# Strassen groups of a two-layer MLP: low parts on VectorE, the square on ScalarE, blocks released one by one

## The chip, the core and the metric

One core of a Trainium2 chip runs the kernel as one program. The time is the device time of one execution in microseconds (us); the median of several executions stands for a kernel. The profile is of one further execution of the same program. Engines: PE is TensorE's matmul, PEld its weight load, DVE VectorE, ACT ScalarE, POOL GpSimd, SP the queue that issues the loads and stores.

## The reference, cut to what matters

A two-layer network works on 512 latent and 256 context tokens of width 1024. Each layer is a mixer (attention, convolution, a state-space part) and then an MLP with 4096 hidden columns. Layer 0 runs the MLP for both token sets, layer 1 for the latent tokens only. All is float32. The part that the change is about:

```
def squared_relu_mlp(t, w1, w2):
    return jnp.square(jax.nn.relu(t @ w1)) @ w2
...
        f_lat = squared_relu_mlp(modulate(rms_norm(h, g_pre_mlp), sh2, sc2), w_mlp_in[l], w_mlp_out[l])
...
            f_ctx = squared_relu_mlp(modulate(rms_norm(hc, g_pre_mlp), sh2c, sc2c), w_mlp_in[l], w_mlp_out[l])
```

The shifts, scales and gates of a layer ("conditioning") come from `c_act @ w_ada[l] + b_ada[l]`, with a matrix of 1024 x 6144.

## The kernel before

**Splitting.** Each float32 operand of a large product is split into a high part, rounded to the matmul's type by a ScalarE cast, and a low part, the difference, by a subtraction. Three matmuls (high-high, high-low, low-high; `mm3`, L638) then stand for one product.

**The MLP** (`phase_mlp`, L1435) takes the hidden columns in 8 groups of 512, which are 4 column blocks of 128. Groups 0 and 7 run plainly. Groups 1 to 6 of both layers (`E.fast`, L1005) run `strassen(g)` (L1457), in four stages:

1. `blocks` and `wload` (L629, L614) load the four blocks of w_mlp_in, two at a time, and split them. Of each two, the first low part is made on VectorE and the second on GpSimd (L624).
2. `up` (L1462) makes 24 matmuls for one block, then relu on ScalarE (L1468) and its square on VectorE (L1470). For context tokens a cast (L1472) and a subtraction (L1473) follow. In layer 0 the four blocks are gone through for the context tokens, and then again for the latent ones.
3. `w2_forms` (L653) loads four rows of w_mlp_out into raw tiles and makes eight forms in layer 0, seven in layer 1: quarters of the matrix, or differences of them (L666) that overwrite the raw quarters. `halves_split` (L644) makes a form's two halves: two casts (L648) and two low parts, one on VectorE and one on GpSimd (L649). `h_forms` (L687) makes seven forms of the hidden values (L696, L697, L703 to L709).
4. Seven products (`times`, L1500) of 12 matmuls each, with two additions to the accumulators after each (L1514). They come in the order l11 r11, l12 r21, s2 t2, s1 t1, s3 t3, s4 r22, l22 t4. In layer 0 the context tokens' plain product (L1488) stands among them.

**Buffers.** The tag "w" has 10 tiles of 4 KB a partition (`E.nw`, L996). Raw loads, split blocks and forms all take them, and so do the conditioning's raw loads (`ada_slice`, L817). In layer 1 the forms r22, t1 and t4, of two tiles each, have six tiles of their own, "wx" (L1454). Relu's output takes one of four tiles "t2", which transposes and the conditioning use too. The tag "B4" has two tiles in the MLP; the state-space preparation uses it in groups 1 to 3 of layer 0.

**Late conditioning.** In groups 4 and 5 of layer 0 two slices of layer 1's conditioning run: four steps after each two blocks of w_mlp_in (`E.ada1`, L1002). A step loads two tiles of 512 KB and makes eight matmuls on each (L825).

**Order.** The program is traced in source order. A scheduling pass then simulates it while it is built, and gives each engine and the SP queue a fixed order: what is ready first goes first, and among ready work what was traced first. At run time every queue keeps that order, and an instruction that waits holds up all that stand behind it on its engine. A tile's release is a wait of the same kind.

Of the kernel before, what the change touches and what calls it, by code (L numbers as in the profile page):

```python
# [7 lines left out]
F32 = mybir.dt.float32  # L8
# [3 lines left out]
AF = mybir.ActivationFunctionType  # L12
OP = mybir.AluOpType
# [597 lines left out]
    return E.wp.tile(shape, dt, name="w", tag="w", bufs=E.nw)  # L611


def wload(E, views):  # L614

    nc = E.nc
    raws, out = [], []
    for v in views:
        raws.append(wtile(E, [P, 1024]))
        nc.sync.dma_start(raws[-1], v)  # L620
    for turn, raw in enumerate(raws):
        hi, lo = (wtile(E, [P, 1024], F32R) for _ in range(2))
        nc.scalar.copy(hi, raw)  # L623
        (nc.gpsimd if turn % 2 and E.wpool else nc.vector).tensor_sub(lo, raw, hi.bitcast(F32))  # L624
        out.append((hi, lo))
    return out


def blocks(E, w, b0, n, k):  # L629

    return [[x.rearrange("p (k c) -> p k c", k=k) for x in hl] for hl in wload(E, [w[b0 + i] for i in range(n)])]


def w_out_load(E, l, half):
# [6 lines left out]
    nc.tensor.matmul(out, ll, rh, start=False, stop=last)  # L641


def halves_split(E, wt, src, turn):  # L644

    hi, lo = (wt([P, 2, 512], F32R) for _ in range(2))
    for i, x in enumerate(src):
        E.nc.scalar.copy(hi[:, i], x)  # L648
        (E.nc.gpsimd if (i + turn) % 2 else E.nc.vector).tensor_sub(lo[:, i], x, hi[:, i].bitcast(F32))  # L649
    return hi, lo  # L650


def w2_forms(E, views, ctx):  # L653


    nc = E.nc
    V = nc.vector
    raw = []
    for v in views:
        raw.append(wtile(E, [P, 1024]))  # L660
        nc.sync.dma_start(raw[-1], v)
    q = {(j, n): [raw[2 * j + i][:, n * 512:(n + 1) * 512] for i in range(2)] for j in range(2) for n in range(2)}

    def sub(o, x, y):
        for i in range(2):
            V.tensor_sub(q[o][i], q[x][i], q[y][i])  # L666

    F = {}
    wx = E.wx if E.nwx else lambda s, d: wtile(E, s, d)
    wt = lambda s, d: wtile(E, s, d)  # L670
    F["r11"] = halves_split(E, wt, q[0, 0], 0)
    F["r21"] = halves_split(E, wt, q[1, 0], 1)
    if ctx:
        F["r12"] = halves_split(E, wt, q[0, 1], 0)
    F["r22"] = halves_split(E, wx, q[1, 1], 1)
    sub((0, 0), (0, 1), (0, 0))
    sub((0, 1), (1, 1), (0, 1))
    sub((1, 1), (1, 1), (0, 0))
    F["t2"] = halves_split(E, wt, q[1, 1], 0)
    F["t1"] = halves_split(E, wx, q[0, 0], 1)  # L680
    sub((1, 0), (1, 0), (1, 1))
    F["t3"] = halves_split(E, wt, q[0, 1], 0)
    F["t4"] = halves_split(E, wx, q[1, 0], 1)
    return F


# [126 lines left out]
def ada_slice(E, a, M, l, s):  # L813
    nc = E.nc
    V = nc.vector
    for kc in range(8):
        raw = [wtile(E, [P, 1024]) for _ in range(2)]  # L817
        for k in range(2):
            c0 = s * 2048 + k * 1024
            nc.sync.dma_start(raw[k], a["w_ada"][l, kc * P:(kc + 1) * P, c0:c0 + 1024])  # L820
        if kc == 0:
            pa = E.pt('a')
        for k in range(2):
            for b in range(4):
                nc.tensor.matmul(pa[32 * b:32 * b + 32, k * 256:(k + 1) * 256], E.cT[:, kc],  # L825
                                 raw[k][:, b * 256:(b + 1) * 256], start=kc == 0 and k == 0, stop=kc == 7,
                                 skip_group_check=True)
        yield
    rows = E.t2([P, 512])
    nc.gpsimd.memset(rows, 0.0)  # L830
    bias = a["b_ada"][l, s * 2048:(s + 1) * 2048].rearrange("(o k b j) -> b o k j", o=1, k=2, b=4)
    for b in range(4):
        nc.sync.dma_start(rows[32 * b:32 * b + 2].rearrange("p (k j) -> p k j", k=2), bias[b].to_broadcast([2, 2, 256]))
    V.tensor_add(rows, rows, pa)
    pt = E.pt('a')
    for q in range(4):
        nc.tensor.transpose(pt[:, q * P:(q + 1) * P], rows[:, q * P:(q + 1) * P], E.ident)
    pv = pt.rearrange("p (k j b w) -> p k j b w", k=2, j=2, b=4)
    for w in range(2):
        V.tensor_copy(M.mod[s][:, w].rearrange("p (k b j) -> p k j b", k=2, b=4), pv[:, :, :, :, w])  # L840
    if s != 1:
        k = 0 if s == 0 else 1
        o = 8 if s == 0 else 0
        V.scalar_tensor_tensor(out=M.A[k], in0=M.mod[s][:, :, o:o + 8], scalar=1.0, in1=bc(M.gpre[:, k], 1, 2),
                               op0=OP.add, op1=OP.mult)
    if s != 0:
        k = s - 1
        gp = E.t2([P, 512])[:, :256]
# [142 lines left out]
def hybrid_kernel(tc, a, out):  # L991
# [40 lines left out]
def block(E, l, cols):  # L1032
# [13 lines left out]
    with psum_phase(E, f"m{l}", m=3, a=1, q=2) as E.pp, \  # L1046
            tc.tile_pool(name=f"mlp{l}", bufs=1, reuse_waits="tile") as E.g4p, \
            tc.tile_pool(name=f"prep{l}", bufs=1, reuse_waits="tile") as E.mp:
        E.ps, E.nb4 = 'a', 2
        E.xa = E.f4  # L1050
        a2 = phase_post(E, l, st)
        return phase_mlp(E, l, a2)


def drain(gen):
# [379 lines left out]
def phase_mlp(E, l, cols):  # L1435
# [15 lines left out]
    ada = ada_steps()  # L1451
    prep = ssm_spill(E) if l == 0 else iter(())

    E.nwx = 0 if both else 6  # L1454
    E.wx = lambda shape, dt: E.g4p.tile(shape, dt, name="wx", tag="wx", bufs=E.nwx)

    def strassen(g):  # L1457
# [4 lines left out]
        def up(c, w, sg):  # L1462
            n, A = (NL, aL) if sg == 0 else (NCX, aC)
            pt = E.pt('m')[:, :n]
            for kc in range(8):
                mm3(nc, pt, w[0][:, kc], w[1][:, kc], A(0, kc), A(1, kc), kc == 0, kc == 7)
            s = E.t2([P, 512])[:, :n]
            nc.scalar.activation(s, pt, AF.Relu)  # L1468
            o = s if sg else hf[c // 2][:, c % 2]
            V.scalar_tensor_tensor(out=o, in0=pt, scalar=0.0, in1=s, op0=OP.max, op1=OP.mult)  # L1470
            if sg:
                nc.scalar.copy(hx[0][:, c], s)  # L1472
                V.tensor_sub(hx[1][:, c], s, hx[0][:, c].bitcast(F32))  # L1473

        w = []
        for k in range(2):
            w.extend(blocks(E, w1, g * 4 + k * 2, 2, 8))
            for _ in range(E.ada1.get(g, 0)):
                next(ada, None)
        for _ in range(E.npr.get(g, 0)):  # L1480
            next(prep, None)
        for sg in ((1, 0) if both else (0,)):
            for c in range(4):
                up(c, w[c], sg)
        R = w2_forms(E, [w2[g * 4 + c] for c in range(4)], both)
        L = h_forms(E, hf)

# [40 lines left out]
    def mlp1(h1, c, w, sg, part=None):  # L1528
# [3 lines left out]
        pt = E.pt('m')[:, :n]  # L1532
        for kc in range(8):
            mm3(nc, pt, w[0][:, kc], w[1][:, kc], A(0, kc, ts), A(1, kc, ts), kc == 0, kc == 7)
        s = E.t2([P, 512])[:, :n]
        nc.scalar.activation(s, pt, AF.Relu)
        V.scalar_tensor_tensor(out=s, in0=pt, scalar=0.0, in1=s, op0=OP.max, op1=OP.mult)
        hi, lo = (h1[sg][q](c)[:, ts] for q in range(2))
# [120 lines left out]
```

## Time and profile before

| what | value |
|---|---|
| median of 3 executions | 1704.34 us (1702.84 to 1710.09) |
| the profiled execution's own time | 1707.07 us |
| span of its profile, first to last instruction | 1705.1 us |
| mean granted TensorE clock, as a share of full speed | 0.952 |
| Strassen groups of layer 0, from the span's start | about 500 to 948 us |
| Strassen groups of layer 1, from the span's start | about 1393 to 1645 us |

In the stretch view each engine has its busy time in the stretch and its number of instructions in brackets; PEclk is the granted clock's mean, and where it is below 1.00 a part of the stretch ran at half speed. In the views by line and in time order, the bracket or the last column is idle time of the engine just ahead of the instruction, and what ended it.

### The profile page before, as it was taken

To read this page: it belongs to the slowest core of one execution; us is meant where nothing else is said; L and a number is where in the kernel's file an instruction comes from. 1 tells how busy PE (TensorE), PEld (TensorE's weight loads), DVE (VectorE), ACT (ScalarE), POOL (GpSimd) and SP (SyncE) were. 2 spreads that over 40 slices of the span, in tenths; PEclk is the share of its full clock that TensorE was granted. 3 is DMA by queue.
4 is the path that set the end of the run, shared out by engine and by line. 5 is a ranking of instruction groups with operands and counts; after the bars stand their busy time and mean duration, and the time that the engine had idled before them with its cause. 6 is when DMAs were issued, how large, how long until landed. Compare 5 with 4: busy or idle time off the path is not lost.

```text
span 1705.1 us, 23175 instructions
## 1 busy us (share of the span) xinstructions
PE 1559.6 (91%) x8728; PEld 1249.1 (73%) x8728; DVE 1124.6 (66%) x2364; ACT 622.7 (37%) x1205; POOL 384.3 (23%) x297
## 2 busy tenths in 40 slices
PE   5999989997999999998999988999898999999997
PEld 2776866676888778676777866687676877777775
DVE  8676447758676974636366476743775658777775
ACT  5312245545413333323233344112554433334342
POOL 0000220122111222213132235003102233333332
PEclk9999999999899999999999998959899899999999
DMA  9465311033140412344420345731303222222232
GB/s 337 154 214 200 118 34 46 1 112 148 42 145 34 139 49 82 149 149 152 146 74 25 112 185 183 282 99 47 109 1 117 81 76 98 99 99 99 99 116 94
DMA packets 72991, 193.83 MB, mean 114 GB/s; under 512 B 15152, under 2 KB 25648, under 8 KB 72496
## 3 DMA queue, kind: packets, MB, share of 16 engines
q1 hardware_dynamic: 72880, 192.37, 32.5%
q8 instruction: 68, 1.11, 0.3%
q14 instruction: 43, 0.35, 0.1%
HBM read 172.15 MB, written 20.19 MB: 113 GB/s over the span
## 4 chain that ended last, share of the span: by engine, by line
PE 67%; DVE 20%; ACT 5%; DMA 4%; issue 2%; POOL 1%; SPq 0%; DVEq 0%; ACTq 0%; POOLq 0%
PE ps_m L639 14%; PE ps_m L640 13%; PE ps_m L641 13%; PE ps_q L1511 3%; PE ps_q L1510 3%; PE ps_q L1509 3%; PE ps_a L825 2%; ACT p L942 2%; PE ps_s L526 2%; PE ps_q L639 2%; DVE w L666 2%; DVE w L649 2%; PE ps_q L640 2%; PE ps_q L641 2%; PE ps_t L967 1%
## 5 line engine op out<-in xcount | busy, mean ns | idle before, releaser
L624 POOL TENSOR_TENSOR w<-w 128x1024 fp32r<-128x1024 f32 x55 | 137.9, 2508 | 376.0 <-ACT w L623 234.7
L623 ACT CAST w<-w 128x1024 fp32r<-128x1024 f32 x124 | 129.6, 1049 | 180.7 <-DMA w<-in_w_mlp_in 44.1
L639 PE MATMUL ps_m<-g,w 128*128 128x256 f32 (+1 forms) x544 | 183.1, 340 | 9.7 <-ACT w L623 3.8
L641 PE MATMUL ps_m<-g,w 128*128 128x256 f32 (+1 forms) x544 | 182.2, 336 | 1.6 <-DVE w L624 1.6
L640 PE MATMUL ps_m<-g,w 128*128 128x256 f32 (+1 forms) x544 | 182.8, 337 | 0.0
L649 POOL TENSOR_TENSOR w<-w 128x512 fp32r<-128x512 f32 x72 | 113.7, 1585 | 284.6 <-ACT w L648 277.9
L639 PE MATMUL ps_m<-f,w 128*128 128x512 f32 (+1 forms) x464 | 170.4, 370 | 1.0 <-DVE f L1140 0.6
L640 PE MATMUL ps_m<-f,w 128*128 128x512 f32 (+1 forms) x464 | 170.1, 367 | 0.0
L641 PE MATMUL ps_m<-f,w 128*128 128x512 f32 (+1 forms) x464 | 169.7, 366 | 0.0
L639 PE MATMUL ps_m<-w,f 128*128 128x512 f32 (+1 forms) x432 | 160.9, 376 | 8.9 <-DVE p L987 4.0
L641 PE MATMUL ps_m<-w,f 128*128 128x512 f32 (+1 forms) x432 | 161.1, 374 | 0.0
L640 PE MATMUL ps_m<-w,f 128*128 128x512 f32 (+1 forms) x432 | 160.0, 372 | 0.0
L1514 DVE TENSOR_TENSOR g<-g,ps_q 128x512 f32<-128x512 f32 x168 | 107.7, 680 | 58.0 <-PE ps_q L1511 57.9
L648 ACT CAST w<-w 128x512 fp32r<-128x512 f32 x144 | 82.4, 618 | 156.6 <-PE ps_m L640 75.0
L624 DVE TENSOR_TENSOR w<-w 128x1024 fp32r<-128x1024 f32 x69 | 84.2, 1222 | 67.3 <-ACT w L623 61.2
L639 PEld LDWEIGHTS ps_m<-g,w 128*128 128x128 f32 x544 | 107.9, 200 | 23.4 <-ACT w L623 4.8
L1510 PE MATMUL ps_q<-w,f 128*128 128x512 f32 x264 | 108.8, 412 | 11.5 <-DVE w L649 7.1
L641 PEld LDWEIGHTS ps_m<-g,w 128*128 128x128 f32 x544 | 108.0, 199 | 13.4 <-DVE w L624 2.7
L1511 PE MATMUL ps_q<-w,f 128*128 128x512 f32 x264 | 108.5, 411 | 8.8 <-DVE f L697 8.8
L640 PEld LDWEIGHTS ps_m<-g,w 128*128 128x128 f32 x544 | 108.4, 199 | 10.4 <-issue 1.2
L1509 PE MATMUL ps_q<-w,f 128*128 128x512 f32 x264 | 107.9, 410 | 7.5 <-ACT f L696 5.3
L649 DVE TENSOR_TENSOR w<-w 128x512 fp32r<-128x512 f32 x72 | 66.7, 926 | 60.5 <-ACT w L648 51.4
(316 smaller groups left out, 3372.2 us busy)
## 6 DMA issues: line engine op xcount, KB each, us to landing
w<-in_w_ada SPq DMA_DIRECT2D x88, 512.0 KB
w<-in_w_mlp_in SPq DMA_DIRECT2D x64, 512.0 KB
w<-in_w_mlp_out SPq DMA_DIRECT2D x64, 512.0 KB
w<-in_w_out SPq DMA_DIRECT2D x16, 512.0 KB
w<-in_w_conv SPq DMA_DIRECT2D x12, 512.0 KB
h_d<-g SPq DMA_DIRECT2D x12, 512.0 KB
w<-in_w_q SPq DMA_DIRECT2D x8, 512.0 KB
f<-h_d SPq DMA_DIRECT2D x8, 512.0 KB
```

What stands on the lines that cost most here:

```text
L526: nc.tensor.matmul(out(g), U[d].o[rows, q, k].rearrange("p t i -> p (t i)"), sp[d][rows, q, k, lo:NCH], start=False, stop=d == 1 and q == ...
L623: nc.scalar.copy(hi, raw)
L624: (nc.gpsimd if turn % 2 and E.wpool else nc.vector).tensor_sub(lo, raw, hi.bitcast(F32))
L639: nc.tensor.matmul(out, lh, rh, start=first, stop=False)
L640: nc.tensor.matmul(out, lh, rl, start=False, stop=False)
L641: nc.tensor.matmul(out, ll, rh, start=False, stop=last)
L648: E.nc.scalar.copy(hi[:, i], x)
L649: (E.nc.gpsimd if (i + turn) % 2 else E.nc.vector).tensor_sub(lo[:, i], x, hi[:, i].bitcast(F32))
L1509: nc.tensor.matmul(o, f[:, 0, c, js], rh[:, c], start=first and c == 0, stop=False, **kw)
L1510: nc.tensor.matmul(o, f[:, 0, c, js], rl[:, c], start=False, stop=False, **kw)
L1511: nc.tensor.matmul(o, f[:, 1, c, js], rh[:, c], start=False, stop=c == 1, **kw)
L1514: V.tensor_add(a_, a_, bank[:, th * 512:(th + 1) * 512])
```

## The change

All low parts of a Strassen group move from GpSimd to VectorE, those of w_mlp_in and those of the forms. The square of relu in a Strassen group is an ACT activation (Square) instead of a VectorE multiplication of the PSUM bank with relu's output. In layer 0, `up` goes block by block: context, then latent. Relu's output has two tiles "relu" of its own, in the plain groups also. The conditioning's raw loads in layer 0's MLP take the two "B4" tiles instead of "w" tiles. "wx" in layer 1 has four tiles instead of six.

```diff
-        (nc.gpsimd if turn % 2 and E.wpool else nc.vector).tensor_sub(lo, raw, hi.bitcast(F32))
+        (nc.gpsimd if turn % 2 and E.wpool and pool else nc.vector).tensor_sub(lo, raw, hi.bitcast(F32))
...
         E.nc.scalar.copy(hi[:, i], x)
-        (E.nc.gpsimd if (i + turn) % 2 else E.nc.vector).tensor_sub(lo[:, i], x, hi[:, i].bitcast(F32))
+        E.nc.vector.tensor_sub(lo[:, i], x, hi[:, i].bitcast(F32))
...
-        raw = [wtile(E, [P, 1024]) for _ in range(2)]
+        raw = [(E.ada_w or wtile)(E, [P, 1024]) for _ in range(2)]
...
         E.ps, E.nb4 = 'a', 2
+        E.ada_w = lambda E, shape: E.mp.tile(shape, F32, name="ada_w", tag="B4", bufs=E.nb4)
         E.xa = E.f4
         a2 = phase_post(E, l, st)
-        return phase_mlp(E, l, a2)
+        cols = phase_mlp(E, l, a2)
+        E.ada_w = None
+        return cols
...
-    E.nwx = 0 if both else 6
+    E.nwx = 0 if both else 4
...
-            s = E.t2([P, 512])[:, :n]
+            s = E.g4p.tile([P, 512], F32, name="relu", tag="relu", bufs=2)[:, :n]
             nc.scalar.activation(s, pt, AF.Relu)
             o = s if sg else hf[c // 2][:, c % 2]
-            V.scalar_tensor_tensor(out=o, in0=pt, scalar=0.0, in1=s, op0=OP.max, op1=OP.mult)
+            nc.scalar.activation(o, s, AF.Square)
...
-            w.extend(blocks(E, w1, g * 4 + k * 2, 2, 8))
+            w.extend(blocks(E, w1, g * 4 + k * 2, 2, 8, False))
...
-        for sg in ((1, 0) if both else (0,)):
-            for c in range(4):
-                up(c, w[c], sg)
+        for c in range(4):
+            if both:
+                up(c, w[c], 1)
+            up(c, w[c], 0)
...
-        s = E.t2([P, 512])[:, :n]
+        s = E.g4p.tile([P, 512], F32, name="relu", tag="relu", bufs=2)[:, :n]
```

## Rows read from the trace of the kernel before

**Rows 1.** The page's head and its busy times: busy us, share of the span.

```profile
span 1705.1 us, 23175 instructions
PE 1559.6 (91%) x8728; PEld 1249.1 (73%) x8728; DVE 1124.6 (66%) x2364; ACT 622.7 (37%) x1205; POOL 384.3 (23%) x297
```

**Rows 2.** Stretches of layer 0's Strassen groups: length, PE, PEld, DVE, ACT, POOL, PEclk, DMA, GB/s.

```profile
553.00:566.00 13.00, 8.79 (x39) 6.20 (x40) 13.00 (x19) 4.63 (x9) 4.71 (x3) 1.00 0.29 92
...
718.00:731.00 13.00, 9.65 (x70) 7.61 (x67) 2.50 (x4) 3.25 (x6) 2.52 (x1) 0.74 0.59 204
...
804.00:813.00 9.00, 6.39 (x45) 5.30 (x37) 1.68 (x3) 2.79 (x4) 2.38 (x1) 0.81 0.59 182
...
861.00:875.00 14.00, 10.62 (x33) 8.18 (x34) 7.32 (x13) 2.28 (x4) 5.39 (x3) 0.76 0.09 30
...
sum 448.00, PE 426.49 PEld 344.69 DVE 280.76 ACT 138.89 POOL 109.06; mean PE 47.39 PEld 38.30 DVE 31.20 ACT 15.43 POOL 12.12
```

**Rows 3.** Four groups of layer 1 as stretches: the undisturbed one, and their sum.

```profile
1540.80:1584.20 43.40, 41.48 (x181) 33.56 (x181) 34.67 (x48) 18.02 (x30) 15.37 (x10) 1.00 0.29 97
...
sum 178.40, PE 170.50 PEld 137.97 DVE 140.12 ACT 72.03 POOL 61.61; mean PE 42.62 PEld 34.49 DVE 35.03 ACT 18.01 POOL 15.40
```

**Rows 4.** PE's matmuls in order of time, inside a product: start, duration (us).

```profile
870.46 0.39 PE L1510 MATMUL ps_q<-w,f 128*128 128x512 f32 x1
...
870.69 0.39 PE L1511 MATMUL ps_q<-w,f 128*128 128x512 f32 x1
```

**Rows 5.** PE's waits from 500 to 948 us: total us, times, longest.

```profile
PE ps_q L1510 <- DVE w L649: 7.1, 9, 1.9
PE ps_q L1510 <- POOL w L649: 4.4, 3, 2.9
```

**Rows 6.** PE's waits from 1393 to 1645 us.

```profile
PE ps_q L1511 <- DVE f L697: 8.8, 7, 1.8
PE ps_q L1509 <- ACT f L696: 5.3, 6, 1.5
```

**Rows 7.** Groups by line and shape, whole trace: count, busy us, mean ns, idle ahead.

```profile
L649 POOL TENSOR_TENSOR w<-w 128x512 fp32r<-128x512 f32 x72 | 113.7, 1585 | 284.6 <-ACT w L648 277.9 <-DVE w L649 5.1 <-POOL w L649 1.1
...
L649 DVE TENSOR_TENSOR w<-w 128x512 fp32r<-128x512 f32 x72 | 66.7, 926 | 60.5 <-ACT w L648 51.4 <-DMA w<-in_w_mlp_out 6.1 <-POOL w L649 2.9
...
L624 DVE TENSOR_TENSOR w<-w 128x1024 fp32r<-128x1024 f32 x69 | 84.2, 1222 | 67.3 <-ACT w L623 61.2 <-PE ps_q L640 5.6 <-issue 0.3
...
L1470 DVE SCALAR_TENSOR_TENSOR f<-ps_m,t 128x512 f32<-128x512 f32 x48 | 32.7, 682 | 42.6 <-ACT t L1468 42.6
...
L717 ACT ACTIVATE dump<-f 128x512 bf16<-128x512 f32 x22 | 13.8, 627 | 3.2 <-DMA f<-in_ctx 2.6 <-DMA f<-in_x 0.5
```

**Rows 8.** In order of time: a GpSimd low part in layer 0, a VectorE difference in layer 1.

```profile
859.33 4.22 POOL L649 TENSOR_TENSOR w<-w 128x512 fp32r<-128x512 f32 x1
...
1503.17 2.64 DVE L705 TENSOR_TENSOR f<-f,f 128x512 f32<-128x512 f32 x1
```

**Rows 9.** The SP queue's loads ahead of the stretch from 718 us.

```profile
707.06 8.12 SPq L820 DMA_DIRECT2D w<-in_w_ada  x8
716.56 2.04 SPq L620 DMA_DIRECT2D w<-in_w_mlp_in  x2
```

**Rows 10.** PE waiting for a conditioning load near the start of the program.

```profile
51.72 0.64 PE L825 MATMUL ps_a<-w,cT 128*32 128x256 f32 x8 [1.19 <-DMA w<-in_w_ada]
```

**Rows 11.** A group's end in layer 1, order of time on ACT and DVE: relu, square, casts.

```profile
1493.06 0.59 ACT L1468 ACTIVATE t<-ps_m 128x512 f32<-128x512 f32 x1
...
1495.19 1.14 ACT L696 CAST f<-f 128x512 fp32r<-128x512 f32 x2
...
1493.98 0.68 DVE L1470 SCALAR_TENSOR_TENSOR f<-ps_m,t 128x512 f32<-128x512 f32 x1
```

**Rows 12.** The first relu of layer 0's plain group 0, and PE behind it.

```profile
432.57 0.66 ACT L1536 ACTIVATE t<-ps_m 128x256 f32<-128x256 f32 x2 [0.47 <-DVE f L785]
...
433.52 0.58 PE L639 MATMUL ps_m<-g,w 128*128 128x256 f32 x1 [1.58 <-DVE t L1537]
```

More of the change, by code (lines that the diff above doesn't have):

```diff
@@ L611, in wtile, with wload @@
     return E.wp.tile(shape, dt, name="w", tag="w", bufs=E.nw)
-def wload(E, views):
+def wload(E, views, pool=True):
     nc = E.nc
@@ L623, in wload, with blocks @@
         nc.scalar.copy(hi, raw)
-        (nc.gpsimd if turn % 2 and E.wpool else nc.vector).tensor_sub(lo, raw, hi.bitcast(F32))
+        (nc.gpsimd if turn % 2 and E.wpool and pool else nc.vector).tensor_sub(lo, raw, hi.bitcast(F32))
         out.append((hi, lo))
     return out
-def blocks(E, w, b0, n, k):
-    return [[x.rearrange("p (k c) -> p k c", k=k) for x in hl] for hl in wload(E, [w[b0 + i] for i in range(n)])]
+def blocks(E, w, b0, n, k, pool=True):
+    return [[x.rearrange("p (k c) -> p k c", k=k) for x in hl]
+            for hl in wload(E, [w[b0 + i] for i in range(n)], pool)]
 def w_out_load(E, l, half):
@@ L641, in mm3, with halves_split @@
     nc.tensor.matmul(out, ll, rh, start=False, stop=last)
-def halves_split(E, wt, src, turn):
+def halves_split(E, wt, src):
     hi, lo = (wt([P, 2, 512], F32R) for _ in range(2))
@@ L670, in w2_forms @@
     wt = lambda s, d: wtile(E, s, d)
-    F["r11"] = halves_split(E, wt, q[0, 0], 0)
-    F["r21"] = halves_split(E, wt, q[1, 0], 1)
+    F["r11"] = halves_split(E, wt, q[0, 0])
+    F["r21"] = halves_split(E, wt, q[1, 0])
     if ctx:
-        F["r12"] = halves_split(E, wt, q[0, 1], 0)
-    F["r22"] = halves_split(E, wx, q[1, 1], 1)
+        F["r12"] = halves_split(E, wt, q[0, 1])
+    F["r22"] = halves_split(E, wx, q[1, 1])
     sub((0, 0), (0, 1), (0, 0))
@@ L678, in w2_forms @@
     sub((1, 1), (1, 1), (0, 0))
-    F["t2"] = halves_split(E, wt, q[1, 1], 0)
-    F["t1"] = halves_split(E, wx, q[0, 0], 1)
+    F["t2"] = halves_split(E, wt, q[1, 1])
+    F["t1"] = halves_split(E, wx, q[0, 0])
     sub((1, 0), (1, 0), (1, 1))
-    F["t3"] = halves_split(E, wt, q[0, 1], 0)
-    F["t4"] = halves_split(E, wx, q[1, 0], 1)
+    F["t3"] = halves_split(E, wt, q[0, 1])
+    F["t4"] = halves_split(E, wx, q[1, 0])
     return F
@@ L1049, in block @@
         E.ps, E.nb4 = 'a', 2
+        E.ada_w = lambda E, shape: E.mp.tile(shape, F32, name="ada_w", tag="B4", bufs=E.nb4)
         E.xa = E.f4
         a2 = phase_post(E, l, st)
-        return phase_mlp(E, l, a2)
+        cols = phase_mlp(E, l, a2)
+        E.ada_w = None
+        return cols
 def drain(gen):
```

## The prediction

> **What bounds the kernel now.** I read the page first: TensorE is busy for 1559.6 of 1705.1 us, 91% [rows 1]. So only what takes away TensorE's waits, or its half-speed stretches behind them, can move the time, and at most there. I then read the Strassen groups as stretches.
>
> Layer 0's take 448.0 us with 426.5 of matmul, so 21.5 us are idle [rows 2]. Three stretches also ran partly at half clock. What half clock costs is the length times one minus PEclk: 13 x 0.26 = 3.4, 9 x 0.19 = 1.7 and 14 x 0.24 = 3.4 us, together 8.5. Layer 0 thus loses 30.0 us, in four parts:
> - 718 to 731: 3.35 idle and 3.4 clock; 804 to 813: 2.6 and 1.7. Together 11.1 us. Both follow a burst of loads: eight conditioning loads are issued from 707.06, and only at 716.56 the second two blocks of w_mlp_in [rows 9]. The conditioning had taken the w tiles.
> - 861 to 875: 3.4 idle and 3.4 clock, 6.8 us. TensorE waits for a GpSimd low part that took 4.22 us where their mean is 1.59 [rows 7, 8].
> - 553 to 566: 4.2 idle, and VectorE is busy for all 13.00 us [rows 2]. That is state-space preparation on top of a group.
> - the rest, 7.9 us, in pieces at the groups' ends. The list of waits names the low parts of forms: 7.1 us behind VectorE, 4.4 behind GpSimd, the 2.9 of the third part among them [rows 5].
>
> Four groups of layer 1 take 178.4 us, 44.6 each; the undisturbed one takes 43.4 with 41.5 of matmul at full clock [rows 3]. So a group loses 3.1 us: (178.4 - 170.5) / 4 = 2.0 idle, and 1.1 of clock. Six groups lose 18.6. The waits are the cast and the low part of a hidden form, at each group's end [rows 6].
>
> **The change, part by part.**
>
> *Low parts to VectorE.* 6 x 8 + 6 x 7 = 90 halves of forms and 24 blocks leave GpSimd. A half costs GpSimd 1.59 us and VectorE 0.93, a block costs VectorE 1.22 [rows 7]. So VectorE takes on 90 x 0.93 + 24 x 1.22 = 113 us at today's means. It gives up the squares: 48 x 0.68 = 33 us, and 24 of half the size, put at half of that, 8. Net +72 us, 6 a group. In layer 1 VectorE is busy 35.0 of 44.6 us [rows 3], so 41 would still fit. I expect less: its 0.93 and the 2.64 us of a difference [rows 8] fall while GpSimd works on the same tiles, and 0.68 is what the same shape takes on a PSUM operand [rows 7]. At 0.68 a half, all 180 halves cost 122 us, against some 90 x 0.93 = 84 for today's ninety, so 38 us more; with the blocks' 29 and the squares' -41 it is 26, two a group. Idle VectorE hides that, but not from 553 to 566, where there is none; for that part I take no gain.
>
> What goes is the GpSimd operation as the last link to a product. For the 861 to 875 hole I take 6.5 of 6.8. Of the 7.9 in pieces I take 3, because the forms still wait for tiles that earlier products hold, and that chain stays.
>
> The Trainium skill, SBUF — State Buffer, section Who interferes with whom, says that a VectorE instruction with two SBUF inputs and a GpSimd instruction that reads SBUF hold a shared port in turn, the second fully blocked. The 4.22 us agree with it. By that rule VectorE's long operations all go with GpSimd's, the whole 7.9 could go too, and the sum below would be 5 us lower; I keep to the rows, which show two such cases.
>
> *Square on ScalarE.* 48 squares at 0.63 us, the nearest row (a square of 128x512 from SBUF), plus 24 at half: 38 us more on an engine that is 37% busy [rows 1, 7], so hidden, but for the last of a group. There relu starts at 1493.06, VectorE's square at 1493.98 ends at 1494.66, and the cast starts at 1495.19 [rows 11], 2.13 us after relu. With the square on the same engine it can start after 0.59 + 0.63 = 1.2 us. The gain is 0.9 us a group at most; ScalarE's order can eat all of it, since casts of forms stand in the same queue.
>
> *Four wx tiles instead of six.* They hold r22, t1 and t4. With four, t4's casts wait for the end of the product s1 t1, and their raw tiles stay taken until then. t4 is wanted two products later: 24 matmuls at 0.23 us [rows 4] are 5.5 us, against two casts and two low parts, some 2.6. So t4 itself isn't late. But t3 then gets its tiles only from r11's, and the next group's first blocks load later by one form's splitting, 2 to 3 us. These blocks fill TensorE's time today while s2 is made. Fewer tiles can only delay, so the one bound is nothing; the other is a hole up to that load: 4.3 us idle and 1.7 of clock, against 3.1 today, +2.9 a group.
>
> For layer 1 I set 0.9 from the square and 1.1 from the low part and the clock against 1.0 for the tiles: -1.0 a group, -6 (bounds -18.6 and +17).
>
> *Blocks one by one.* In layer 0 the first block is free after its own 24 context and 24 latent matmuls rather than after the context pass over all four, and the last one at the same moment. No wait of rows 5 names these; I cost it at nothing, covered by the matmuls of the other blocks. It has no effect in layer 1.
>
> *Conditioning in B4 tiles.* The second two blocks no longer queue for tiles behind eight loads, so the 11.1 us should go. In exchange a conditioning load waits for the matmuls on the load two before, and TensorE, whose order is fixed, for the load. There are 32. Nearest row: 1.19 us waited for one such load [rows 10]. Bounds 0 and 32 x 1.19 = 38; with both loads of a step in flight, and two whole groups of other matmuls to spread them over (718 to 861 us today and more), I take 2. Net -9.
>
> *Relu tiles.* Group 0's first relu waits for a tile of the transposes, and TensorE 1.58 us behind it [rows 12]; layer 1 begins alike. Between 0 and -3.2; I take -1, as the square there stays behind VectorE's own queue.
>
> **Sum:** -6.5 - 3 - 6 - 9 - 1 = -25.5 us. The profiled execution's own time is 1707.07, 2.0 above its span and 2.7 above the median. That gives 1681.6 beside it, and 1678.8 beside the median of 1704.34. I say 1679.
>
> **Rivals.**
>
> *Layer 1 gives back what layer 0 gains.* The four wx tiles cost their full +2.9 a group, +17 us; layer 0 gains 18.5 and group 0 one. Net -2.5: 1702. For it: layer 1's holes sit just where a tile comes late. Against it: seven products of slack. The Trainium skill, Perfetto Trace Analysis, section Optimization Strategy, says that the same gap repeating on the engine that should be saturated can mean too few buffers for the next tile. By that rule the edit goes the wrong way in layer 1, where the gap does repeat [rows 3, 6]; no row shows six tiles against four. Chance 0.17.
>
> *Slower: the SP queue.* A conditioning load that waits for its B4 tile at the head of SP's queue holds every load behind it. Six times in groups 4 and 5 weights stand behind such loads (two pairs of w_mlp_in and the four of w_mlp_out in each). If each makes a hole as from 718 to 731, 6.75 us, they cost 40 instead of 11.1, so +29; with -16.5 from the other terms it is +13: 1717. It decides once a B4 tile comes free later than the load behind is wanted. Against it: a tile is held for eight matmuls of 0.64 us together [rows 10]. Chance 0.10.
>
> *The order isn't as meant.* The pass could still put conditioning first, and the 11.1 stay: -16, 1688. And VectorE may be full in the three preparation groups, +2 to +6 each: 1685 to 1697. Both lie on the faster side, in the forecast's 0.73.
>
> **How the numbers follow.** Some 0.5%, 8.5 us, is what a measurement of this kernel can tell from no change: faster is below 1695.8, slower above 1712.9. The forecast and its weaker forms have 0.73, the first rival 0.17, the second 0.10. At best all 30.0, 18.6 and 3.2 go, 1653, which I don't expect whole: low end 1657. The high end takes in the first rival: 1704.
>
> **What would show it.** Right: no GpSimd work in the Strassen stretches; halves at 0.68 us on VectorE; no hole behind the conditioning loads; PEclk 1.00 from 861 to 875's counterpart; layer 1's groups near 43.5 us. Wrong: TensorE waiting for conditioning loads or, in layer 1, for a VectorE difference, t4 or the next block; SP waiting on B4 in groups 4 and 5; groups of layer 1 above 45 us.

## The result, and the profile after

| | before | after |
|---|---|---|
| median (runs) | 1703.59 us (4: 1699.36 to 1710.09) | 1681.30 us (4: 1676.95 to 1683.63) |
| ratio, 95% interval | | 0.9863, 0.9824 to 0.9902 |
| profiled execution, its span | 1707.07, 1705.1 us | 1679.50, 1677.6 us |

The change is faster by 1.4%: 22 us between the medians, 27.5 between the two spans. The predicted 1679 lies 2.3 us beside the measured median. How the 27.5 us are composed is another matter, and most of what follows is about that.

The page of after, head and two groups of its costliest (line, engine, operation, count, busy us, mean ns, idle ahead):

```profile
span 1677.6 us, 22956 instructions
PE 1546.1 (92%) x8728; PEld 1235.4 (74%) x8728; DVE 1101.0 (66%) x2406; ACT 659.1 (39%) x1277; POOL 185.8 (11%) x183
...
L650 DVE TENSOR_TENSOR w<-w 128x512 fp32r<-128x512 f32 x144 | 93.5, 685 | 81.9 <-ACT w L649 81.9
```

GpSimd's work has halved [rows 1], and a half's low part takes VectorE 685 ns now instead of 926 [rows 7]. TensorE's busy time fell by 13.5 us although its 8728 matmuls are the same: the mean granted clock rose from 0.952 to 0.965.

To see where the time went I cut both spans at the same events: where the MLP begins (the mixer's last projection is copied out), the first and the last addition of a Strassen product, and the first projection of layer 1. In the stretch view (length, PE, PEld, DVE, ACT, POOL with instructions, PEclk, DMA, GB/s), the kernel before, and then after:

```profile
368.79:544.44 175.65, 162.79 (x921) 141.41 (x920) 121.42 (x321) 64.58 (x126) 37.28 (x29) 0.94 0.30 107
544.44:1048.75 504.31, 471.53 (x2472) 377.46 (x2470) 320.20 (x594) 169.81 (x303) 137.08 (x94) 0.97 0.33 115
1291.35:1405.87 114.52, 101.55 (x518) 85.75 (x516) 71.39 (x136) 45.26 (x83) 34.10 (x23) 0.93 0.26 94
1405.87:1705.10 299.23, 274.94 (x1164) 221.87 (x1164) 223.37 (x316) 111.08 (x183) 97.40 (x57) 0.97 0.29 101
```

```profile
367.64:532.76 165.12, 158.62 (x916) 138.86 (x915) 115.82 (x317) 66.90 (x132) 28.49 (x26) 0.98 0.32 114
532.76:1013.75 480.99, 465.40 (x2476) 372.44 (x2474) 312.38 (x609) 191.35 (x346) 39.10 (x36) 0.99 0.35 121
1251.38:1358.64 107.26, 98.76 (x517) 83.69 (x515) 70.13 (x137) 45.28 (x84) 20.91 (x14) 0.95 0.28 100
1358.64:1677.64 319.00, 280.32 (x1164) 223.10 (x1164) 215.71 (x344) 124.24 (x207) 18.77 (x11) 0.96 0.28 94
```

The four are the start of layer 0's MLP (with plain group 0), its Strassen groups with group 7 and the tail, the start of layer 1's MLP, and its Strassen groups to the end. They changed by -10.5, -23.3, -7.3 and **+19.8** us, together -21.3. The other 6.2 lie in mixers (1.2 and 0.1) and in layer 1's first projections (4.9), which the diff does not touch; in the kernels below those projections took anything from 89.9 to 98.2 us, so I put no cause to them.

TensorE's waits in the Strassen groups of after (total us, times, longest), layer 0 and then layer 1, against [rows 5, 6]:

```profile
PE ps_a L347 <- DVE f L341: 1.2, 1, 1.2
PE ps_q L1516 <- DVE w L650: 1.1, 1, 1.1
PE ps_m L640 <- ACT w L623: 0.6, 2, 0.4
...
PE ps_m L640 <- ACT w L623: 19.0, 6, 3.2
PE ps_q L1517 <- DVE f L698: 7.0, 6, 1.2
```

In layer 0 a few short waits are left, 2.9 us in all. In layer 1 a wait has appeared that the kernel before did not have there: six times, once a group, TensorE waits 3.2 us for the cast of the next block of w_mlp_in. A middle group as a stretch, and the sum of four:

```profile
1456.40:1504.30 47.90, 43.53 (x180) 34.49 (x180) 33.68 (x52) 20.26 (x33) 0.00 (x0) 0.96 0.26 88
...
sum 191.60, PE 174.05 PEld 138.52 DVE 135.26 ACT 80.85 POOL 0.00; mean PE 43.51 PEld 34.63 DVE 33.82 ACT 20.21 POOL 0.00
```

A group takes 47.9 us, 3.3 more than the mean of [rows 3]; (191.6 - 174.05) / 4 = 4.4 are idle, against 2.0. In order of time, on PE, ACT and the SP queue:

```profile
1451.55 0.39 PE L1515 MATMUL ps_q<-w,f 128*128 128x512 f32 x1
...
1462.20 0.50 PE L640 MATMUL ps_m<-g,w 128*128 128x512 f32 x1 [3.21 <-ACT w L623]
...
1452.57 0.59 ACT L1473 ACTIVATE relu<-ps_m 128x512 f32<-128x512 f32 x1
1453.19 0.63 ACT L1475 ACTIVATE f<-relu 128x512 f32<-128x512 f32 x1
1453.85 1.14 ACT L697 CAST f<-f 128x512 fp32r<-128x512 f32 x2
...
1461.10 1.04 ACT L623 CAST w<-w 128x1024 fp32r<-128x1024 f32 x1 [5.07 <-DMA w<-in_w_mlp_in]
...
1457.58 0.93 SPq L620 DMA_DIRECT2D w<-in_w_mlp_in  x2
```

Read it from the bottom: the load goes out at 1457.58, 6.0 us after the group's first product began (1451.55); the cast waits for it, and TensorE for the cast. What the load waits for is the low part of a form, as SP's waits from 1445 to 1460 us say:

```profile
SPq L620 <- DVE w L650: 23.3, 2, 23.1
```

The square and the cast behind relu come fast here: the cast starts 1.28 us after relu (1452.57 to 1453.85), so the 3.21 us are not its doing.

In the kernel before, the same load leaves at 1494.71, in a group whose last block's square starts at 1493.98 [rows 11]:

```profile
1494.71 0.80 SPq L620 DMA_DIRECT2D w<-in_w_mlp_in  x2
...
1498.00 1.05 ACT L623 CAST w<-w 128x1024 fp32r<-128x1024 f32 x1 [1.67 <-DMA w<-in_w_mlp_in]
```

There the cast starts 4.9 us after the relu of 1493.06; in after 8.5 us after the one of 1452.57. So the mechanism of my first rival happened in layer 1, while the total is that of the forecast. Something else must have paid for it, and the experiments had to find what.

### The profile page after: what moved, and what is told of

It is laid out like the page before. It is cut to its first block, busy times and chain, and to the rows that moved or that the text cites. A ratio compares the mean times of both kernels' runs of the same rounds, so it can differ in the third digit from the quotient of the medians.

```text
span 1677.6 us, 22956 instructions
## 1 busy us (share of the span) xinstructions
PE 1546.1 (92%) x8728; PEld 1235.4 (74%) x8728; DVE 1101.0 (66%) x2406; ACT 659.1 (39%) x1277; POOL 185.8 (11%) x183
## 4 chain that ended last, share of the span: by engine, by line
PE 72%; DVE 16%; ACT 5%; DMA 5%; issue 2%; POOL 1%; SPq 0%; DVEq 0%; ACTq 0%; POOLq 0%
PE ps_m L640 15%; PE ps_m L642 14%; PE ps_m L641 14%; PE ps_q L1515 4%; PE ps_q L1516 4%; PE ps_q L1517 4%; PE ps_a L826 3%; ACT p L943 2%; DMA w<-in_w_mlp_in 2%; PE ps_q L641 2%; PE ps_q L640 2%; PE ps_s L526 2%; PE ps_q L642 2%; DMA w<-in_w_ada 1%; DVE p L935 1%
## 5 line engine op out<-in xcount | busy, mean ns | idle before, releaser
L624 DVE TENSOR_TENSOR w<-w 128x1024 fp32r<-128x1024 f32 x93 | 115.6, 1244 | 113.1 <-ACT w L623 81.9
L624 POOL TENSOR_TENSOR w<-w 128x1024 fp32r<-128x1024 f32 x31 | 76.2, 2458 | 804.6 <-ACT w L623 422.4
L650 DVE TENSOR_TENSOR w<-w 128x512 fp32r<-128x512 f32 x144 | 93.5, 685 | 81.9 <-ACT w L649 81.9
L640 PEld LDWEIGHTS ps_m<-g,w 128*128 128x128 f32 x544 | 105.8, 197 | 38.6 <-ACT w L623 23.9
L642 PEld LDWEIGHTS ps_m<-g,w 128*128 128x128 f32 x544 | 107.2, 197 | 11.3 <-issue 1.2
L641 PEld LDWEIGHTS ps_m<-g,w 128*128 128x128 f32 x544 | 106.3, 196 | 12.3 <-issue 2.1
L1517 PE MATMUL ps_q<-w,f 128*128 128x512 f32 x264 | 104.5, 396 | 7.0 <-DVE f L698 7.0
L1515 PE MATMUL ps_q<-w,f 128*128 128x512 f32 x264 | 105.5, 402 | 0.6
L1516 PE MATMUL ps_q<-w,f 128*128 128x512 f32 x264 | 104.4, 395 | 1.2 <-DVE w L650 1.1
L640 PEld LDWEIGHTS ps_m<-f,w 128*128 128x128 f32 x464 | 89.1, 193 | 20.5 <-issue 6.6
```

The lines of the kernel that those rows point to most:

```text
L624: (nc.gpsimd if turn % 2 and E.wpool and pool else nc.vector).tensor_sub(lo, raw, hi.bitcast(F32))
L640: nc.tensor.matmul(out, lh, rh, start=first, stop=False)
L641: nc.tensor.matmul(out, lh, rl, start=False, stop=False)
L650: E.nc.vector.tensor_sub(lo[:, i], x, hi[:, i].bitcast(F32))
L1515: nc.tensor.matmul(o, f[:, 0, c, js], rh[:, c], start=first and c == 0, stop=False, **kw)
L1516: nc.tensor.matmul(o, f[:, 0, c, js], rl[:, c], start=False, stop=False, **kw)
```

## The experiments

All kernels compute the whole result. In the table each stretch is cut as above; ratios are to the kernel before on the same chip. Four of the kernels have the same code in layer 0 (after, wx6_relu1, wx6_t2, wx6_sq_dve): their layer 0 groups took 481.0, 481.8, 480.8 and 480.9 us, so a stretch repeats to about 1 us. Where a stretch is unchanged but scheduled anew, as layer 1's in the runs that edit layer 0 alone, it moves by up to 3; layer 1's first projections, above, move by 8.

| kernel | median us | ratio (95%) | start L0 | groups L0 | start L1 | groups L1 to end |
|---|---|---|---|---|---|---|
| before | 1703.59 | 1 | 175.6 | 504.3 | 114.5 | 299.2 |
| after | 1681.30 | 0.9863 (0.9824 to 0.9902) | 165.1 | 481.0 | 107.3 | 319.0 |
| wx6_relu1 | 1664.66 | 0.9756 (0.9727 to 0.9785) | 165.2 | 481.8 | 107.5 | 299.8 |
| wx6_t2 | 1668.37 | 0.9773 (0.9742 to 0.9804) | 165.1 | 480.8 | 110.4 | 302.1 |
| before_wx4 | 1742.62 | 1.0214 (1.0177 to 1.0252) | 175.6 | 505.4 | 115.1 | 336.3 |
| undo_relu | 1696.40 | 0.9946 (0.9914 to 0.9977) | 175.1 | 482.9 | 110.3 | 317.5 |
| undo_ada | 1678.40 | 0.9841 (0.9820 to 0.9863) | 165.1 | 479.4 | 108.7 | 317.7 |
| undo_order | 1687.44 | 0.9893 (0.9863 to 0.9922) | 166.2 | 483.9 | 108.9 | 317.7 |
| undo_pool | 1691.05 | 0.9921 (0.9893 to 0.9950) | 167.1 | 484.8 | 111.4 | 327.7 |
| undo_square | 1685.85 | 0.9883 (0.9861 to 0.9905) | 165.1 | 487.0 | 108.8 | 316.0 |
| undo_order_ada | 1690.28 | 0.9897 (0.9858 to 0.9936) | 167.7 | 495.6 | 107.3 | 316.1 |
| undo_order_ada_pool | 1705.76 | 0.9993 (0.9963 to 1.0023) | 166.6 | 498.4 | 111.6 | 323.6 |
| before_relu | 1685.35 | 0.9865 (0.9835 to 0.9895) | 167.2 | 500.6 | 110.6 | 297.7 |
| wx6_sq_dve | 1671.93 | 0.9793 (0.9764 to 0.9821) | 165.1 | 480.9 | 108.4 | 306.7 |

**1. Are the four wx tiles the hole in layer 1?** Six again in the changed kernel. To make room for them in layer 1, one run keeps a single relu tile there (no run has two beside six wx tiles), in both places where the tile is taken, and another takes relu's output from "t2" in layer 1, as before.

```diff
-    E.nwx = 0 if both else 4
+    E.nwx = 0 if both else 6
...
-            s = E.g4p.tile([P, 512], F32, name="relu", tag="relu", bufs=2)[:, :n]
+            s = E.g4p.tile([P, 512], F32, name="relu", tag="relu", bufs=2 if both else 1)[:, :n]
```

> The changed kernel with six wx tiles in layer 1 again; to make room, relu has one tile of its own there instead of two. Theory A (the four wx tiles make layer 1's longer groups: t4 waits for the end of the product s1 t1, its raw tiles stay taken, the next w_mlp_in load is issued 6.0 us after a group's first product instead of 2.7): the 3.2 us waits for a w_mlp_in cast go, layer 1's groups fall from 47.9 to 43 to 45 us, the kernel to 1657 to 1667 us. Theory B (the longer groups come from the low parts on VectorE and the square on ScalarE, which stand in those queues ahead of the next blocks): the groups stay near 47.9 and the time within 4 us of 1681.

```diff
-    E.nwx = 0 if both else 4
+    E.nwx = 0 if both else 6
...
-            s = E.g4p.tile([P, 512], F32, name="relu", tag="relu", bufs=2)[:, :n]
+            s = (E.g4p.tile([P, 512], F32, name="relu", tag="relu", bufs=2) if both else E.t2([P, 512]))[:, :n]
```

> The changed kernel with six wx tiles, and in layer 1 relu's output in the shared t2 tiles as before, so that layer 1's buffers are those of the kernel before. Theory A: groups of 43 to 45 us as in the other run with six. Theory C (relu's own tiles shorten the start of each layer's MLP, where group 0's relu waited for a tile of the transposes; in layer 1 they are worth 7 us): this one is 5 to 8 us slower than the other run with six tiles. If C is wrong the two agree within 3 us.

And the cut alone, in the kernel before:

```diff
-    E.nwx = 0 if both else 6
+    E.nwx = 0 if both else 4
```

> The kernel before with nothing changed but four wx tiles instead of six. Theory A: layer 1's groups go from 44.6 to 47 to 49 us, the kernel to 1718 to 1725. Theory B: groups and time stay, 1700 to 1708.

With six tiles layer 1's groups take 299.8 us instead of 319.0, and wx6_relu1 is the fastest kernel of this study, 2.4% under the kernel before. Its waits from layer 1's Strassen groups on, and after them those of before_wx4:

```profile
PE ps_q L1515 <- ACT f L697: 9.6, 6, 2.0
PE ps_q L1517 <- DVE f L698: 4.0, 6, 0.9
...
```

```profile
PE ps_m L639 <- ACT w L623: 22.4, 6, 4.3
PE ps_q L1511 <- DVE f L697: 15.0, 12, 2.6
...
```

The wait for w_mlp_in's cast is gone in the one and has come in the other, six times; in before_wx4 nothing but the number of tiles was changed. The cut costs 19.2 us of layer 1's groups in the changed kernel and 37.0 in the kernel before. The other edits thus make up about half of it. My rival's +17 was right for the first; for the second I expected 14 to 21, and 37 is about twice that. The relu tile in layer 1 is worth 3.7 us between the two runs with six tiles, 2.9 of them in the start of its MLP: less than theory C's 5 to 8. The intervals of the two ratios overlap, so it is the stretch that shows it.

**2. What pays for it: undo one part at a time.** Relu's output in "t2" again (the first line in both places where the tile is taken), the conditioning's loads in "w" tiles, or all context columns before the latent ones:

```diff
-            s = E.g4p.tile([P, 512], F32, name="relu", tag="relu", bufs=2)[:, :n]
+            s = E.t2([P, 512])[:, :n]
```

> The changed kernel with relu's output in the shared t2 tiles again, in both layers and in all groups. Theory C: the stretch from the last first-half projection of the mixer to the first Strassen product loses what it won, 10 us in layer 0 and 7 in layer 1: 1694 to 1700 us. Rival (those stretches are shorter because of a different order or clock that the tiles have no part in): within 4 us of 1681.

```diff
-        raw = [(E.ada_w or wtile)(E, [P, 1024]) for _ in range(2)]
+        raw = [wtile(E, [P, 1024]) for _ in range(2)]
```

> The changed kernel with the late conditioning's loads in the shared w tiles again. If their place in the w tiles made the two holes of 11.1 us in groups 4 and 5 of layer 0: 1688 to 1694 us, with TensorE waiting for a w_mlp_in cast in both groups. Rival (going block by block needs the second two blocks so much later that the loads no longer matter): within 4 us of 1681, no such waits.

```diff
-        for c in range(4):
-            if both:
-                up(c, w[c], 1)
-            up(c, w[c], 0)
+        for sg in ((1, 0) if both else (0,)):
+            for c in range(4):
+                up(c, w[c], sg)
```

> The changed kernel with layer 0's blocks gone through for all context tokens first, then for the latent ones, as before. Prediction: nothing, within 4 us of 1681. Rival (a block freed early lets the w_mlp_out rows and their forms in early, and that is what emptied layer 0's holes): 1687 to 1697 us, with waits for low parts of forms in layer 0.

The relu tiles are worth 15 us, 10.0 of them in the start of layer 0's MLP and 3.0 in that of layer 1. That is the largest gain of a part undone alone, and I had put it at 1. The rows of the kernel before show it, TensorE first and then ACT:

```profile
426.01 1.12 PE L770 MATMUL ps_q<-ident,g 128*128 128x128 f32 x4 [4.43 <-ACT g L743]
...
424.81 1.15 ACT L743 ACTIVATE g<-g,rs 128x1024 f32<-128x1024 f32 x1 [1.80 <-DVE rs L606]
```

TensorE stands for 4.43 us before the latent tokens' transposes, waiting for their norm, and the first relu of group 0 comes only at 432.57, behind them [rows 12]. Undoing the tiles brings that wait back (TensorE in undo_relu from 400 to 450 us); the list of after for that time does not have it:

```profile
PE ps_q L771 <- ACT g L744: 4.4, 1, 4.4
```

In after the first relu starts at 416.73, between two transposes:

```profile
416.73 0.64 ACT L1542 ACTIVATE relu<-ps_m 128x256 f32<-128x256 f32 x2
417.25 0.56 ACT L779 ACTIVATE t<-ps_q,mod,A 128x256 f32<-128x256 f32 x1
```

With a tile of its own, group 0's context work no longer queues behind the transposes for a "t2" tile, and its matmuls fill the wait. The same 50 us, before from 400 and after from 398:

```profile
400.00:450.00 50.00, 37.15 (x238) 33.02 (x236) 35.65 (x94) 22.94 (x48) 15.38 (x14) 0.80 0.24 85
```

```profile
398.00:448.00 50.00, 44.09 (x336) 41.49 (x334) 45.18 (x113) 26.56 (x56) 18.15 (x17) 0.97 0.27 96
```

98 more matmuls fit in. 50 x (0.97 - 0.80) = 8.5 us of TensorE's time there are clock: before, 2 x 50 x 0.20 = 20 us ran at 1.2 GHz, most of them in one piece: TensorE was in waits between 418 and 434 us, and from 424 to 438 every stretch of 2 us has PEclk 0.50. In after 3 us did.

Undoing the conditioning's tiles costs nothing (1678.4, and 479.4 us for the groups of layer 0); undoing the order costs 6 us, 2.9 in layer 0's groups, no more than a stretch moves by, and the rest mostly where the code is the same. Neither brings back the 11.1 us of holes behind the conditioning loads. That would make my -9 worthless, or the two parts do the same thing twice.

**3. Low parts and square, undone.** Every second low part on GpSimd again (in `halves_split` and `blocks`); or the square on VectorE:

```diff
-        E.nc.vector.tensor_sub(lo[:, i], x, hi[:, i].bitcast(F32))
+        (E.nc.gpsimd if (i + turn) % 2 else E.nc.vector).tensor_sub(lo[:, i], x, hi[:, i].bitcast(F32))
...
-            w.extend(blocks(E, w1, g * 4 + k * 2, 2, 8, False))
+            w.extend(blocks(E, w1, g * 4 + k * 2, 2, 8))
```

> The changed kernel with every second low part of the blocks and forms on GpSimd again. If the GpSimd operation as last link was worth what the prediction says (6.5 and 3 us in layer 0, about 1 us a group in layer 1): 1692 to 1700 us, with waits for GpSimd low parts in layer 0. Rival (the order by blocks and the freed tiles already gave the forms time enough): within 4 us of 1681.

```diff
-            nc.scalar.activation(o, s, AF.Square)
+            V.scalar_tensor_tensor(out=o, in0=pt, scalar=0.0, in1=s, op0=OP.max, op1=OP.mult)
```

> The changed kernel with relu's square on VectorE again. Prediction: at most 0.9 us a group in layer 1, so 1681 to 1687 us. Rival (VectorE is then full at the groups' ends, the more so with all low parts on it): 1690 us or more.

GpSimd's share of the low parts costs 10 us: 3.9 in layer 0's groups and 8.7 in layer 1's, with 2.0 and 4.2 in the two starts, less 7.4 us in layer 1's projections and mixer, where the code is the same. The two engines' durations in that run:

```profile
L650 POOL TENSOR_TENSOR w<-w 128x512 fp32r<-128x512 f32 x72 | 104.5, 1457 | 326.3 <-ACT w L649 326.3
...
L650 DVE TENSOR_TENSOR w<-w 128x512 fp32r<-128x512 f32 x72 | 63.5, 882 | 97.6 <-ACT w L649 97.5
```

VectorE's mean for the same operation is 882 ns beside GpSimd and 685 alone, as predicted. The square on VectorE costs 6.0 us in layer 0's groups and saves 3.0 in layer 1's: with four wx tiles its place on ScalarE is no gain there. In undo_square a group's cast starts later (2.68 us behind relu, 1457.90 to 1460.58, against 1.28 in after), but the next block's load leaves sooner (3.8 us behind relu, at 1461.67, against 5.0). TensorE's wait for that block's cast falls from 19.0 to 4.4 us over the six groups, and a wait of 9.1 us for the hidden form's cast comes in its place.

**4. Do order and conditioning tiles replace each other?** Both undone together, and then with GpSimd's low parts as well (the diffs are those above).

> The changed kernel with two of its parts undone together: in layer 0 all context columns of a group first and then the latent ones, as before, and the conditioning's raw loads in w tiles again. Each undone alone cost layer 0's Strassen stretch -1.5 and +3.2 us (386.0 us in the changed kernel, 404.5 before). Theory A: either part alone is enough to free w tiles early, so with both undone the 11.1 us of holes behind the conditioning loads return: Strassen stretch of layer 0 at 395 to 399 us, with waits of TensorE for the cast of a w_mlp_in block near two bursts of conditioning loads; the kernel some 10 us slower than the changed one plus the 1 to 3 us that the lone order cost, 1692 to 1698. Theory B: the low parts on VectorE removed the holes, not the release of tiles: the stretch stays at 386 to 390 and the kernel at 1683 to 1689.

> As the run with order and conditioning tiles undone together, and with every second low part of blocks and forms on GpSimd again as well. What is left of the change then is the square on ScalarE, the relu tiles and the four wx tiles. Theory A (the prediction's account of layer 0: 11.1 for the tiles, 9.5 less 2 for the low parts): layer 0's Strassen stretch comes back to 402 to 406 us, and the kernel to 1700 to 1708 with layer 1's loss of 9 from GpSimd as in the run that undid the low parts alone. Theory B (low parts on GpSimd cost nothing in layer 0, as that run showed a stretch of 384.8): the stretch is that of the run with order and conditioning undone within 2 us.

The first run's two holes, as stretches:

```profile
708.00:722.00 14.00, 10.18 (x75) 7.59 (x75) 2.88 (x3) 3.81 (x7) 0.00 (x0) 0.76 0.61 227
792.00:804.00 12.00, 7.85 (x58) 5.02 (x55) 2.87 (x3) 3.29 (x5) 0.00 (x0) 0.72 0.61 218
```

Idle 3.8 and 4.2 us, clock 14 x 0.24 and 12 x 0.28, 3.4 each: 14.7 us, and the stretch is 14.6 longer than in after. Theory A holds, though both its ranges are just missed, with 400.4 us for the Strassen stretch alone against 395 to 399 and a kernel of 1690 against 1692 to 1698: either part alone empties w tiles in time, and only without both do the holes come back. The SP queue shows it, first in this run, then in after:

```profile
700.21 6.26 SPq L821 DMA_DIRECT2D w<-in_w_ada  x5
707.38 1.80 SPq L620 DMA_DIRECT2D w<-in_w_mlp_in  x2
```

```profile
694.33 3.55 SPq L821 DMA_DIRECT2D ada_w<-in_w_ada  x2
701.19 0.81 SPq L620 DMA_DIRECT2D w<-in_w_mlp_in  x2
```

With GpSimd's low parts on top, layer 0's groups grow by only 2.8 us more, to 498.4, and layer 1's by 7.5; the kernel is then where the kernel before is (0.9993). Theory A's 402 to 406 for the Strassen stretch alone is missed: it took 398.3 (400.4 without GpSimd), theory B's value. The 2.8 us thus lie behind the last Strassen addition.

**5. The relu tiles alone, in the kernel before.** Two in layer 0, one in layer 1:

```diff
-    E.nwx = 0 if both else 6
+    E.nwx, E.nrelu = (0, 2) if both else (6, 1)
...
-            s = E.t2([P, 512])[:, :n]
+            s = E.g4p.tile([P, 512], F32, name="relu", tag="relu", bufs=E.nrelu)[:, :n]
```

> The kernel before with one part of the change: relu's output has tiles of its own, two in layer 0 and one in layer 1 (a second one there does not fit beside six wx tiles); squares, low parts, order and conditioning as before. Theory A: the 10.5 us that the stretch before layer 0's Strassen groups lost, and the 7.2 us of layer 1's, come from the relu tiles alone: stretches of 165 and 107 to 110 us in place of 175.6 and 114.5, the rest as before, the kernel at 1685 to 1692. Theory B: they also need the square or the low parts off the engines they were on: gains under 6 us in sum, 1697 to 1704. My prediction had 1 us for them, bounds 0 and 3.2.

```profile
365.73:532.98 167.25, 159.79 (x921) 139.52 (x920) 120.72 (x319) 63.81 (x126) 37.71 (x32) 0.98 0.31 113
```

This one edit gives 0.9865: as much as the whole change. The other parts together are worth nothing on top of it, because what they gain in layer 0's groups (19.6 us from before_relu to after) the four wx tiles take back in layer 1's (21.3). Of its 27.6 us of span (23 between the medians) 8.4 come from the start of layer 0's MLP (the line above) and 3.9 from that of layer 1, 3.8 from layer 0's groups and 1.5 from layer 1's; the other 10.0 lie where the code is the same. Theory A, with the squares and low parts where they were.

**6. The square of layer 1 on VectorE, with six wx tiles.** Against wx6_relu1:

```diff
-            nc.scalar.activation(o, s, AF.Square)
+            if both:
+                nc.scalar.activation(o, s, AF.Square)
+            else:
+                V.scalar_tensor_tensor(out=o, in0=pt, scalar=0.0, in1=s, op0=OP.max, op1=OP.mult)
```

> The fastest kernel so far (the changed one with six wx tiles and one relu tile in layer 1, 1664.7 us) with the square of layer 1's Strassen groups on VectorE again; layer 0 is the same. Theory A: in layer 1 the square on ScalarE waits behind two casts of forms in ScalarE's fixed order and gains nothing; on VectorE it starts 0.9 us after relu, so a group ends 0.5 us sooner: Strassen stretch of layer 1 and end together 296 to 299 us in place of 299.8, kernel 1661 to 1664. Theory B: the prediction's 0.9 us a group for the square on ScalarE holds although the order eats part of it, or VectorE, with all low parts, has no room: 302 to 306 us, kernel 1667 to 1671.

306.7 us against 299.8: theory B and a little beyond it, 6.9 us for the square, 1.15 a group. A group's end on ACT and DVE in wx6_relu1, and then in wx6_sq_dve:

```profile
1582.94 0.59 ACT L1473 ACTIVATE relu<-ps_m 128x512 f32<-128x512 f32 x1
1583.43 1.12 ACT L649 CAST w<-w 128x512 fp32r<-128x512 f32 x2
1584.45 0.63 ACT L1475 ACTIVATE f<-relu 128x512 f32<-128x512 f32 x1
1585.12 1.14 ACT L697 CAST f<-f 128x512 fp32r<-128x512 f32 x2
...
1586.47 1.28 DVE L698 TENSOR_TENSOR f<-f,f 128x512 fp32r<-128x512 f32 x2
```

```profile
1543.68 0.59 ACT L1473 ACTIVATE relu<-ps_m 128x512 f32<-128x512 f32 x1
...
1545.72 1.14 ACT L697 CAST f<-f 128x512 fp32r<-128x512 f32 x2
...
1544.58 0.68 DVE L1478 SCALAR_TENSOR_TENSOR f<-ps_m,relu 128x512 f32<-128x512 f32 x1
...
1548.18 1.28 DVE L698 TENSOR_TENSOR f<-f,f 128x512 fp32r<-128x512 f32 x2
```

From relu to the cast it is 2.18 us with the square on ScalarE and 2.04 with it on VectorE, 2.13 in [rows 11]: nothing is won there, because with six wx tiles ScalarE's order puts two casts of forms between relu and square (1583.43), which it does not do in after. But the low part behind the cast (L698) starts 3.5 us after relu in the first and 4.5 in the second, where VectorE has the square and all low parts in one queue. With six tiles the square's gain is the room that it leaves on VectorE, not a shorter chain on ScalarE.

## Why the prediction was right, and where it was not

Three of the kernels form a ladder between before and after, each with more parts of the change. Its steps, in the four stretches (us):

| step | start L0 | groups L0 | start L1 | groups L1 |
|---|---|---|---|---|
| relu tiles (before to before_relu) | -8.4 | -3.8 | -3.9 | -1.5 |
| square on ScalarE, four wx tiles and a second relu tile in layer 1 (to undo_order_ada_pool) | -0.6 | -2.2 | +1.0 | +25.9 |
| low parts on VectorE (to undo_order_ada) | +1.1 | -2.8 | -4.3 | -7.5 |
| order and conditioning tiles (to after) | -2.6 | -14.6 | 0 | +2.9 |

The sum was right because one term that was too hopeful and one that was far too small cancel. By stretches, I forecast -18.5 us for layer 0's groups, -6 for layer 1's and -1 for the two starts; measured are -23.3, +19.8 and -17.8, and -6.2 where nothing was changed. That these add up to my number is luck. Three of the signs of being wrong that I had named came true: in layer 1 a wait for the next block and groups above 45 us, and SP waiting on B4. By the prediction's own steps:

- **Low parts, layer 0 (-6.5 and -3).** Halves at 0.68 us on VectorE: measured 0.685. The gain was mis-sized: 2.8 us on the ladder, 3.9 by undoing, against 9.5, and none of it lies between the first and the last Strassen addition, where I had priced it (384.8 us in undo_pool, 386.0 in after). The step that failed is the hole of 861 to 875. GpSimd's 4.22 us operation is no accident of one profile: before_wx4, which has the same layer 0, shows the slow pair again, and the same 2.9 us wait of TensorE for it.

```profile
865.16 6.16 POOL L649 TENSOR_TENSOR w<-w 128x512 fp32r<-128x512 f32 x2 [3.95 <-ACT w L648]
```

  But before_relu and undo_order_ada_pool keep GpSimd's low parts and have no such wait: the longest for a GpSimd low part is 1.4 us in either, as in undo_pool. A cost that a new order removes was put down to the engine. VectorE's 685 ns against 882 beside GpSimd agree with the Trainium skill's rule on the shared port (SBUF — State Buffer, section Who interferes with whom); the 5 us that I would have added to the gain by it did not come in layer 0.
- **Low parts, layer 1 (in the 1.1 a group).** Here the gain is 7.5 us on the ladder and 8.7 by undoing, 1.3 to 1.5 a group. That holds with four wx tiles alone; the last section has six.
- **Square on ScalarE (0.9 a group).** The short chain came in after: square 0.62 us and cast 1.28 us behind relu, against 2.13 to the cast in [rows 11]. It bought nothing there, since the group's end waits for the next block's load: -0.5 a group, no more than stretches move by. With six tiles "ScalarE's order can eat all of it" came true, 2.18 us, and the gain came by another way, the room on VectorE: 1.15 a group. That this is near 0.9 is luck.
- **Four wx tiles (-1.0 a group all in all, bounds +17).** This is the wrong step. I took 1.0 for the tiles, from the argument that t4 is wanted two products later; the text named the right chain itself (the next group's blocks load later by one form's splitting) and then priced it near nothing. Measured: 19.2 us, 3.2 a group; rival 1 had +2.9. Layer 1's groups as a whole came out beyond even my bound of +17. The Trainium skill's rule that spoke against it (Perfetto Trace Analysis, section Optimization Strategy: the same gap repeating can mean too few buffers) agrees with before_wx4, where that edit alone makes six such gaps, 22.4 us in sum. That rival deserved more than 0.17 for its half in layer 1.
- **Blocks one by one (0) and conditioning tiles (-9).** Together -14.6, and the holes behind the conditioning loads did go. But either alone does it: beside undo_order_ada's 495.6 us, layer 0's groups take 483.9 with the tiles alone (-11.7, near the 11.1 that I priced) and 479.4 with the order alone (-16.2). So undo_ada costs nothing, and "I cost it at nothing" for the blocks was wrong, because no wait in the list named a block where the tile's release was what counted. The 2 us that I kept back for waits on conditioning loads did not come: no such wait stands in after's list for layer 0.
- **Relu tiles (-1, bounds 0 to -3.2).** Mis-sized by far: 15.1 us by undoing, 13.0 of them in the two starts (of 17.8 that these lost in all). I priced the wait that the row names, 1.58 us [rows 12], and did not look at what the tile's lateness did to the order: TensorE's 4.43 us wait ahead of it and the half clock behind it belonged to the same cause. Even my bound was a bound on the named wait alone.
- **Rival 2, SP's queue.** SP did wait at its head on B4 tiles, as that rival said, for long:

```profile
SPq L821 <- PE ps_a L826: 109.4, 22, 41.8
```

  That is after from 660 to 860 us: 22 waits, one of 41.8 us, and TensorE's list for layer 0 has no wait for a conditioning load and only 0.6 us for a cast of w_mlp_in. The order put the loads that are wanted sooner ahead, as at 701.19 above.

What stays open: why four wx tiles cost 37 us in the kernel before and 19 in the changed one was read from their waits, not taken apart further (in before_wx4 the load leaves 7.5 us behind the group's last relu, 1561.10 to 1568.58, and in after 5.0; waits of 15.0 us for low parts of hidden forms come on top). And layer 1's groups are shortest in before_relu (297.7), with GpSimd's low parts, VectorE's square and six tiles, though wx6_relu1 is only 2.1 us behind, less than such stretches move by. That layer 1 together with after's layer 0 was not tried.

## What to carry to other kernels

Price a shared buffer by what the order would be without it, not by the wait that a row names: the wait of 1.58 us for a relu tile stood for 10 us at the start of one MLP, because the fixed order could not place ready matmuls in TensorE's gaps. Cutting a rotating buffer is paid in every group by the load at the end of the chain that it holds, so follow the chain to that load's issue and landing (here 6.0 us from the group's first product to the issue, and 3.5 more until the cast could start), not to the next use of the tile's own data. And undo parts in pairs before calling one worthless: two edits that free the same tiles each looked nearly worthless when undone alone (nothing and 2.9 us of layer 0's groups) and were worth 14.6 us together.

## What the runs showed that I had not expected

- An engine's queue that waits long at its head need not cost anything: SP's 41.8 us.
- Moving work to a faster engine depended on the buffers. With four wx tiles VectorE's low parts gain 7.5 us in layer 1; with six, and the square on VectorE in both, layer 1's groups are 8.9 us longer with them than without (wx6_sq_dve 306.7 against before_relu 297.7), and the square's move to ScalarE brings back 6.9. Together the two moves then gain nothing in layer 1.
